# Token tiles transposed in chunks of two, three and four, with the first value projection following them, in a hybrid attention step

## The chip, the cores and the metric

The kernel runs on one core of a Trainium2 chip. The metric is the device time of one execution in microseconds; less is better.

## The reference

One decoder layer for a prompt of 1024 tokens with 16 meta tokens ahead of it, and for 8 samples of 4 new tokens each; 2048 features, all in 32-bit floats. Cut to what matters here, with the head of the layer in full:

```python
def rms_norm(x, g):
    var = mean(x * x, axis=-1)
    return x * rsqrt(var + 1e-6) * g

h = rms_norm(x, norm_pre_g)            # 16 + 1024 + 32 = 1072 tokens x 2048
u = h @ w_in                           # q, k, v, gate of 8 heads; q, k, v, gate, decay of 4 linear heads
...                                    # stick-breaking attention (prompt and paged samples),
...                                    # gated linear attention, SiLU gates
y = x + rms_norm(mixed @ w_out, norm_post_g)
```

The outputs are y for prompt and samples, the new keys and values, and the new linear states. The change is in how h is made, transposed and split, and in the value projection of the first attention head, `h @ w_in[:, 2048:2176]`.

## The kernel before

Every product with `w_in` is done in three matmuls with operands rounded to the fast 32-bit matmul format: a tensor is split into a rounded part (`hh`, `wh`) and the rest (`hl`, `wl`), and the products `wh*hh`, `wh*hl` and `wl*hh` are accumulated. The stationary operand is a weight block of 128 features by 128 outputs, the moving one is `h` transposed: features on partitions, tokens along columns. So `h` must first be normalized with tokens on partitions, and then transposed on TensorE.

The 1072 tokens are nine tiles: x0 (16 meta tokens and 112 of the prompt), x1 to x7 (128 each), x8 (the last 16 of the prompt and the 32 of the samples, with the two halves of the features on different partitions of one buffer). A tile is loaded as two halves of 1024 features (`load_x`, L198 on; 11 buffers) and normalized (`norm_x`, L217 on): ScalarE squares it with a running sum (L227; halves of 1024 for tiles 0 to 4, pieces of 512 after them, 256 for x8), VectorE adds the partial sums (L229), then `rstd_` (L154 on) takes the root: one VectorE operation, Ln and Exp on ScalarE (L162, L163), and four VectorE operations that refine it (L164 to L167). L238 scales the two halves in place.

The head then runs over three chunks of tokens, `CHUNKS`, of three tiles each. In each chunk, for each of the 16 blocks k of features, TensorE transposes the three tiles' blocks into one PSUM bank (`tx`, L262, five banks), ScalarE evacuates it, multiplied by the gain `gpre`, as `hh` (L263), and VectorE evacuates the rest as `hl` (L264). After a chunk's loop the 48 matmuls of the first head's value projection on the chunk follow in the program (L274 to L276), into one of three accumulators, `first`. Their token chunks, `SCHUNKS`, are 378, 378 and 316 columns, cut at multiples of 126 as the attention wants them, and stay within what has been transposed so far. The table `NORMS` places a tile's `norm_x` behind a step (c, k): x3 behind (0, 1), x4 behind (0, 4), x5 (0, 10), x6 (1, 2), x7 (1, 5), x8 (1, 8).

The weights of that projection come in four chunks of 256 KB (`weight_chunk`): ScalarE casts a chunk (L185, L182), VectorE subtracts (L187, L183). The raw chunks share two buffers with those of all later projections.

The order on each engine is drawn up at compile time by a list scheduler that goes by program order and its own estimate of when operands are there. Blocks marked `urgent()` (loads, casts, copies out of accumulators) go ahead of the rest. Each engine then works through its list in order and waits where an operand is late. Loads go through SP's queue and in small part ScalarE's, each of them in order too; eight semaphores take turns in telling of a load's landing, so that a load waits until the one eight before it has landed. `gpre` is a transposed load of 2048 single elements on ScalarE's queue, and the sixth load issued.

After the head, `head(0)` copies the three accumulators to staging tiles `vraw` (L613), which are written out later, and `inproj` runs the key and query projections, attention, the other heads and so on.

Of the kernel before, what the change touches and what calls it, by code (L numbers as in the profile page):

```python
# [20 lines left out]
P = 128  # L21
# [61 lines left out]
def hybrid_step(ctx: ExitStack, tc: tile.TileContext, x_prompt, x_sample, cache_k, cache_v, state_gla,  # L83
# [7 lines left out]
    def urgent():  # L91
        return tc.high_priority(offset=URGENT)
# [16 lines left out]
    def stage(nm, dt=F32):  # L109
        return stg.tile([P, 384], dt, tag="stg", name=nm)  # L110
# [44 lines left out]
    def rstd_(pl, ssq, n, rows, w, nm):  # L155

        v = pl.tile([P, w], F32, tag="rs_v", name=f"v_{nm}")
        r = pl.tile([P, w], F32, tag="rs_r", name=f"r_{nm}")
        t = pl.tile([P, w], F32, tag="rs_t", name=f"t_{nm}")
        v, r, t = v[:rows], r[:rows], t[:rows]  # L160
        vec.tensor_scalar(v, ssq, 1.0 / n, EPS, ALU.mult, ALU.add)
        act.activation(r, v, AF.Ln)  # L162
        act.activation(r, r, AF.Exp, scale=-0.5)  # L163
        vec.tensor_tensor(t, r, r, ALU.mult)  # L164
# [8 lines left out]
    hl = [t[:, 1088:1088 + T] for t in hT]  # L173


    def weight_chunk(w, kk, c0, nm, dst=None):
        with urgent():
            raw = wp.tile([P, 4, P], F32, tag="wr", name=f"wr_{nm}")
            nc.sync.dma_start(raw[:], w[kk * 512:(kk + 1) * 512, c0:c0 + P].rearrange("(k p) c -> p k c", p=P))
            wh, wl = dst or [wp.tile([P, 4, P], F32R, tag=t, name=f"{t}_{nm}") for t in ("wh", "wl")]  # L180
            if dst is None:
                act.copy(wh[:], raw[:])  # L182
                vec.tensor_tensor(wl[:], raw[:], wh[:].bitcast(F32), ALU.subtract)  # L183
                return [(wh[:, k, :], wl[:, k, :]) for k in range(4)]
            act.copy(wh, raw[:])  # L185
            for i in range(2):
                vec.tensor_tensor(wl[i][:], raw[:, 2 * i:2 * i + 2], wh[:, 2 * i:2 * i + 2].bitcast(F32), ALU.subtract)  # L187
        return [(wh[:, k, :], wl[k // 2][:, k % 2, :]) for k in range(4)]
# [3 lines left out]
    with tc.tile_pool(name="xp", bufs=2) as xp, tc.tile_pool(name="xps", bufs=5, space=PSUM) as xps:  # L192
        wf = xp.tile([P, 12, P], F32R, tag="wf", bufs=1, name="wf")
        wfl = [stg.tile([P, 2, P], F32R, tag="stg", name=f"wfl{kk}") for kk in range(6)]
        first = [accp.tile([P, 512], F32, tag="acc", name=f"acc_v0_{c}") for c in range(3)]
        wchunks = []
        xts = {}

        def load_x(i):

            xt = [xp.tile([P, H], F32, tag="x", bufs=11, name=f"x{i}_{f}") for f in range(2 if i < 8 else 1)]
            if i == 8:
                pool.memset(xt[0][32:64], 0.0)
            with urgent():
                for f in range(2):
                    fs = slice(f * H, (f + 1) * H)
                    if i == 0:
                        nc.scalar.dma_start(xt[f][:META], meta_tokens[:, fs])
                        nc.sync.dma_start(xt[f][META:], x_prompt[0, 0:P - META, fs])
                    elif i == 8:  # L210
                        nc.scalar.dma_start(xt[0][64 * f:64 * f + 16], x_prompt[0, SEQ - 16:SEQ, fs])
                        nc.sync.dma_start(xt[0][64 * f + 16:64 * f + 48], x_sample.rearrange("b t d -> (b t) d")[:, fs])
                    else:
                        nc.sync.dma_start(xt[f][:], x_prompt[0, i * P - META:(i + 1) * P - META, fs])
            xts[i] = xt

        def norm_x(i):  # L217
            xt = xts[i]
            rows = P if i < 8 else 112
            w = H if i < 5 else 512 if i < 8 else 256  # L220
            q = len(xt) * H // w
            ssq = xp.tile([P, 4], F32, tag="ssq", name=f"ssq{i}")
            for e in range(q):
                j0 = 0 if i < 5 else (448 if i < 8 else 768) + 1088 * (e % 2)
                jk = hT[15][:rows, j0:j0 + w]
                xe = xt[e * w // H][:rows, e * w % H:e * w % H + w]
                act.activation(jk, xe, AF.Square, accum_out=ssq[:rows, e:e + 1])  # L227
            sq = xp.tile([P, 1], F32, tag="sq", name=f"sq{i}")
            vec.tensor_reduce(sq[:rows], ssq[:rows, :q], mybir.AxisListType.X, ALU.add)  # L229
            if i == 8:  # L230
                other = xp.tile([P, 1], F32, tag="so", bufs=1, name="so")
                pool.memset(other[:], 0.0)
                vec.tensor_copy(other[0:48], sq[64:112])
                vec.tensor_copy(other[64:112], sq[0:48])
                vec.tensor_tensor(sq[:rows], sq[:rows], other[:rows], ALU.add)
            r = rstd_(xp, sq[:rows], D, rows, 1, f"x{i}")
            for t in xt:
                vec.tensor_scalar(t[:rows], t[:rows], r, None, ALU.mult)  # L238

        NORMS = {(0, 1): 3, (0, 4): 4, (0, 10): 5, (1, 2): 6, (1, 5): 7, (1, 8): 8}  # L240
        for i in range(5):
            load_x(i)
            if i == 2:
                constants()
                for kk in range(NK // 4):
                    dst = (wf[:, 4 * kk:4 * kk + 4, :], wfl[2 * kk:2 * kk + 2]) if kk < 3 else None
                    wchunks.extend(weight_chunk(w_in[0], kk, C_SV, f"v0_{kk}", dst))
        for i in range(3):
            norm_x(i)
        for c, (lo, hi) in enumerate(CHUNKS):  # L250
            n = hi - lo
            for k in range(NK):
                ps = xps.tile([P, 384], F32, tag="tx", name=f"tx{c}_{k}")
                ks = slice(k % 8 * P, (k % 8 + 1) * P)
                for j in range(3):
                    xt = xts[3 * c + j]
# [5 lines left out]
                    nc.tensor.transpose(ps[:, j * P:min((j + 1) * P, n)], src, ii)  # L262
                act.activation(hh[k][:, lo:hi], ps[:, :n], AF.Copy, scale=gpre[:, k:k + 1])  # L263
                vec.scalar_tensor_tensor(hl[k][:, lo:hi], ps[:, :n], gpre[:, k:k + 1], hh[k][:, lo:hi].bitcast(F32),  # L264
                                         ALU.mult, ALU.subtract)
                if c == 0 and k == 7:
                    load_x(5)
                if (c, k) in NORMS:
                    norm_x(NORMS[c, k])
            lo, hi = SCHUNKS[c]  # L270
            o_ = first[c][:, :hi - lo]
            for k in range(NK):
                wh, wl = wchunks[k]
                mm(o_, wh, hh[k][:, lo:hi], start=(k == 0), stop=False)  # L274
                mm(o_, wh, hl[k][:, lo:hi], start=False, stop=False)
                mm(o_, wl, hh[k][:, lo:hi], start=False, stop=(k == NK - 1))  # L276
            if c == 0:
                for i in (6, 7, 8):
                    load_x(i)

    def inproj(c0, evac, lo0, nm, chunks=CHUNKS):

# [191 lines left out]
    with tc.tile_pool(name="sp", bufs=1) as sp, tc.tile_pool(name="sps", bufs=1, space=PSUM) as sps:  # L474
# [135 lines left out]
        def head(h):  # L610
# [999 lines left out]
```

## Time and profile before

| | |
|---|---|
| median of 3 runs | 2091.61 us (2091.23 to 2092.55) |
| profiled execution | 2091.43 us |
| its span | 2089.6 us |
| TensorE (PE) busy in the span | 2050.1 us, 98% |
| VectorE (DVE) | 1554.0 us, 74% |
| ScalarE (ACT) | 962.7 us, 46% |
| DMA | 301.86 MB, 144 GB/s on average |

The span is what the profiler sees of the core; 1.8 us of the execution's time lie around it. Times of rows are in microseconds from the span's start. L numbers are lines of the kernel before. PE is TensorE's matmul side, PEld its weight loads, which overlap it; a matmul's row has its own duration, so that back-to-back matmuls overlap in the rows and their spacing is what one costs. "[1.72 <-ACT wf L185]" at a row's end means that the engine stood idle for 1.72 us before it, and what ended that.

### The profile page before, as it was taken

How to read it: one execution, taken by the hardware profiler on the slowest of the kernel's cores; microseconds unless marked ns; L12 is line 12 of the kernel's file. 1: busy time of each engine (PE TensorE's matmuls, PEld its weight loads, DVE VectorE, ACT ScalarE, POOL GpSimd, SP SyncE). 2: the span in 40 equal slices, each digit the busy share in tenths (PEclk: the TensorE clock that was granted, in tenths of full speed). 3: DMA queues.
4: the chain of work that ended last, by engine and by line, in shares of the span. 5: the costliest groups of instructions: out<-in, count | busy, mean ns of one | idle time of the engine just before them, and what ended most of it. 6: DMA issues, size and time to landing. Idle time of an engine off the chain costs nothing.

```text
span 2089.6 us, 42075 instructions
## 1 busy us (share of the span) xinstructions
PE 2050.1 (98%) x12546; PEld 1863.7 (89%) x12546; DVE 1554.0 (74%) x6299; ACT 962.7 (46%) x2304; POOL 84.3 (4%) x303
## 2 busy tenths in 40 slices
PE   5999999999999999999999999999999999999998
PEld 4999999999999998999899998998888897777776
DVE  6368889889888989899798887978444347553576
ACT  7345555565655556433535335353433325432332
POOL 0012000001000000000000000000000000000000
PEclk9999999999999999999999999999999999999999
DMA  6245554545554442533333434335777666442385
GB/s 204 78 139 150 145 151 137 168 129 153 144 157 142 138 126 77 144 95 85 107 98 81 118 78 115 90 85 159 229 238 227 224 215 194 137 151 75 129 280 186
DMA packets 374910, 301.86 MB, mean 144 GB/s; under 512 B 46488, under 2 KB 315192, under 8 KB 374680
## 3 DMA queue, kind: packets, MB, share of 16 engines
q1 hardware_dynamic: 372344, 298.64, 48.3%
q8 instruction: 99, 1.62, 0.3%
q14 instruction: 131, 1.07, 0.2%
q10 hardware_dynamic: 2336, 0.53, 0.1%
HBM read 241.75 MB, written 57.31 MB: 143 GB/s over the span
## 4 chain that ended last, share of the span: by engine, by line
PE 85%; DVE 8%; DMA 4%; issue 2%; ACT 1%; SPq 0%; POOL 0%; DVEq 0%; ACTq 0%; POOLq 0%
PE acc_g L292 5%; PE acc_g L293 5%; PE acc_g L294 5%; PE b L1517 4%; PE b L1518 4%; PE b L1519 4%; PE acc_k L292 3%; PE acc_k L293 3%; PE acc_k L294 3%; PE acc_v L292 3%; PE acc_q L292 3%; PE acc_q L293 3%; PE acc_q L294 3%; PE acc_v L294 3%; PE acc_v L293 3%; DVE jk L411 2%
## 5 line engine op out<-in xcount | busy, mean ns | idle before, releaser
L411 DVE SCALAR_TENSOR_TENSOR jk<-kp,qb 128x128 f32<-128x128 f32 x2048 | 591.7, 289 | 42.5 <-DMA qb<-qsd 1.5
L292 PE MATMUL acc_g<-hT,wh_g 128*128 128x368 f32 (+2 forms) x768 | 251.1, 327 | 0.0
L293 PE MATMUL acc_g<-hT,wh_g 128*128 128x368 f32 (+2 forms) x768 | 247.4, 322 | 0.0
L294 PE MATMUL acc_g<-hT,wl_g 128*128 128x368 f32 (+2 forms) x768 | 247.0, 322 | 0.0
L1517 PE MATMUL b<-ring,f 128*128 128x512 f32 x416 | 166.0, 401 | 4.0 <-DVE u L1399 1.6
L1335 DVE TENSOR_TENSOR ring<-wr,ring 128x512 fp32r<-128x512 f32 x104 | 70.7, 690 | 132.0 <-ACT ring L1334 131.6
L411 DVE DVE_READ_ACCUMULATOR jk<-kp,qb 128x1 f32 x2048 | 166.3, 81 | 0.0
L1518 PE MATMUL b<-ring,f 128*128 128x512 f32 x416 | 162.8, 391 | 0.3 <-DVE ring L1335 0.2
L1519 PE MATMUL b<-ring,f 128*128 128x512 f32 x416 | 162.9, 392 | 0.0
L292 PEld LDWEIGHTS acc_g<-hT,wh_g 128*128 128x128 f32 x768 | 144.3, 188 | 12.3 <-issue 10.6
L293 PEld LDWEIGHTS acc_g<-hT,wh_g 128*128 128x128 f32 x768 | 144.4, 188 | 1.5 <-issue 0.8
L294 PEld LDWEIGHTS acc_g<-hT,wl_g 128*128 128x128 f32 x768 | 144.3, 188 | 0.4 <-DVE wl_g L183 0.3
L1334 ACT CAST ring<-wr 128x512 fp32r<-128x512 f32 x104 | 64.2, 621 | 167.5 <-DMA wr<-in_w_out_dram 74.1
L292 PE MATMUL acc_gv<-hT,wh_gv 128*128 128x384 f32 (+1 forms) x384 | 129.9, 338 | 0.0
L292 PE MATMUL acc_k<-hT,wh_k 128*128 128x378 f32 (+1 forms) x384 | 127.6, 332 | 0.0
L293 PE MATMUL acc_k<-hT,wh_k 128*128 128x378 f32 (+1 forms) x384 | 125.4, 326 | 0.0
L292 PE MATMUL acc_q<-hT,wh_q 128*128 128x368 f32 (+2 forms) x384 | 125.4, 326 | 0.0
L294 PE MATMUL acc_k<-hT,wl_k 128*128 128x378 f32 (+1 forms) x384 | 125.2, 326 | 0.0
L294 PE MATMUL acc_gv<-hT,wl_gv 128*128 128x384 f32 (+1 forms) x384 | 124.5, 324 | 0.0
L293 PE MATMUL acc_gv<-hT,wh_gv 128*128 128x384 f32 (+1 forms) x384 | 124.5, 324 | 0.0
L293 PE MATMUL acc_q<-hT,wh_q 128*128 128x368 f32 (+2 forms) x384 | 123.6, 322 | 0.0
L294 PE MATMUL acc_q<-hT,wl_q 128*128 128x368 f32 (+2 forms) x384 | 123.5, 322 | 0.0
(441 smaller groups left out, 5301.7 us busy)
## 6 DMA issues: line engine op xcount, KB each, us to landing
kp<-in_cache_k_dram SPq DMA_DIRECT2D x512, 64.0 KB
vr<-in_cache_v_dram SPq DMA_DIRECT2D x64, 512.0 KB
tf<-in_w_out_dram SPq DMA_DIRECT2D x64, 256.0 KB
td<-tf SPq DMA_DIRECT2D x64, 256.0 KB
qb<-qsd SPq DMA_DIRECT2D x64, 256.0 KB
wr_g<-in_w_in_dram SPq DMA_DIRECT2D x64, 256.0 KB
wr<-td SPq DMA_DIRECT2D x64, 256.0 KB
wr<-in_w_out_dram SPq DMA_DIRECT2D x48, 256.0 KB
```

Of the source, the lines that this page charges most:

```text
L292: mm(acc[c][:, :n], wh, hh[k][:, lo:hi], start=(k == 0), stop=False)
L293: mm(acc[c][:, :n], wh, hl[k][:, lo:hi], start=False, stop=False)
L294: W.mark = mm(acc[c][:, :n], wl, hh[k][:, lo:hi], start=False, stop=(k == NK - 1)).ins
L411: ins = vec.scalar_tensor_tensor(jk[:], kp[:], 1.0, qbs[h, b][:, t, :], ALU.mult, ALU.mult, accum_out=zt[:, t, NPG - 1 - i:NPG - i])
L1334: act.copy(wh, r)
L1335: vec.tensor_tensor(wl, r, wh.bitcast(F32), ALU.subtract)
L1517: mm(bk[:], ah, wh, start=first and k == 0, stop=False, skip_group_check=True)
L1518: mm(bk[:], ah, wl, start=False, stop=False, skip_group_check=True)
L1519: mm(bk[:], al, wh, start=False, stop=last and k == 7, skip_group_check=True)
```

## The change

`XCHUNKS` takes the place of `CHUNKS` in the head: tiles (0, 1), (2, 3, 4), (5, 6, 7, 8), that is 256, 384 and 432 columns. The first head's value accumulators have these widths too, and are put together to the chunks of 126 in the copies to `vraw`, five copies for three. A token tile gets 13 half-tile buffers for 11. The raw tiles of the first two weight chunks get buffers of their own, and the first chunk's cast is put behind tile x1's root. The loads are issued in another order: x0, x1, weight chunk 0, x2, chunk 1, x3, chunks 2 and 3, x4, the constants, x5, then x6 behind step (0, 7) and x7 and x8 behind (0, 15).

In `norm_x` all squares are taken on a half of 1024 features (x8: its one buffer); x0's second half is squared by VectorE, and x1's squares stand behind x0's root. The root is shorter: two VectorE operations add the partial sums with the mean's factor and epsilon, Ln and Exp follow, two more VectorE operations make the correction, and the scaling multiplies by the raw root and the correction in one instruction. `NORMS` places x2 behind (0, 1), x3 (0, 6), x4 (0, 11), x5 (1, 1), x6 (1, 4), x7 (1, 8), x8 (1, 11). x0 and x1 are normalized ahead of the chunks.

```diff
+TILES = [(0, 1), (2, 3, 4), (5, 6, 7, 8)]
+XCHUNKS = [(0, 2 * 128), (2 * 128, 5 * 128), (5 * 128, T)]
...
-    def weight_chunk(w, kk, c0, nm, dst=None):
+    def weight_chunk(w, kk, c0, nm, dst=None, raw=None, behind=None):
         with urgent():
-            raw = wp.tile([P, 4, P], F32, tag="wr", name=f"wr_{nm}")
+            if raw is None:
+                raw = wp.tile([P, 4, P], F32, tag="wr", name=f"wr_{nm}")
...
-            act.copy(wh, raw[:])
+            ins = act.copy(wh, raw[:]).ins
+            if behind is not None:
+                tc.add_manual_dep(ins, behind.name, NOSYNC, reason="behind")
...
-            xt = [xp.tile([P, H], F32, tag="x", bufs=11, name=f"x{i}_{f}") for f in range(2 if i < 8 else 1)]
+            xt = [xp.tile([P, H], F32, tag="x", bufs=13, name=f"x{i}_{f}") for f in range(2 if i < 8 else 1)]
...
-            w = H if i < 5 else 512 if i < 8 else 256
-            q = len(xt) * H // w
-            ssq = xp.tile([P, 4], F32, tag="ssq", name=f"ssq{i}")
+            q = len(xt)
+            ssq = xp.tile([P, 2], F32, tag="ssq", name=f"ssq{i}")
+            jk = hT[15][:].rearrange("p (a x) -> p a x", a=2)[:rows, :, 576:1088]
             for e in range(q):
-                j0 = 0 if i < 5 else (448 if i < 8 else 768) + 1088 * (e % 2)
-                jk = hT[15][:rows, j0:j0 + w]
-                xe = xt[e * w // H][:rows, e * w % H:e * w % H + w]
-                act.activation(jk, xe, AF.Square, accum_out=ssq[:rows, e:e + 1])
-            sq = xp.tile([P, 1], F32, tag="sq", name=f"sq{i}")
-            vec.tensor_reduce(sq[:rows], ssq[:rows, :q], mybir.AxisListType.X, ALU.add)
+                x, s = xt[e][:rows], ssq[:rows, e:e + 1]
+                if i == 0 and e == 1:
+                    vec.scalar_tensor_tensor(hT[14][:, 0:H], x, 1.0, x, ALU.mult, ALU.mult, accum_out=s)
+                else:
+                    ins = act.activation(jk, x.rearrange("p (a x) -> p a x", a=2), AF.Square, accum_out=s).ins
+                    if i == 1:
+                        tc.add_manual_dep(ins, roots[0].name, NOSYNC, reason="behind")
...
-            r = rstd_(xp, sq[:rows], D, rows, 1, f"x{i}")
-            for t in xt:
-                vec.tensor_scalar(t[:rows], t[:rows], r, None, ALU.mult)
-
-        NORMS = {(0, 1): 3, (0, 4): 4, (0, 10): 5, (1, 2): 6, (1, 5): 7, (1, 8): 8}
...
+            vec.tensor_scalar(t, ssq[:rows, 0:1], 1.0 / D, EPS, ALU.mult, ALU.add)
+            vec.scalar_tensor_tensor(v, second, 1.0 / D, t, ALU.mult, ALU.add)
+            act.activation(g, v, AF.Ln)
+            roots.append(act.activation(g, g, AF.Exp, scale=-0.5).ins)
+            vec.scalar_tensor_tensor(t, g, v, g, ALU.mult, ALU.mult)
+            vec.tensor_scalar(t, t, -0.5, 1.5, ALU.mult, ALU.add)
+            for x in xt:
+                vec.tensor_scalar(x[:rows], x[:rows], g, t, ALU.mult, ALU.mult)
+
+        def load_w(kk):
+            dst = (wf[:, 4 * kk:4 * kk + 4, :], wfl[2 * kk:2 * kk + 2]) if kk < 3 else None
+            raw = xp.tile([P, 4, P], F32, tag="wx", name=f"wx{kk}") if kk < 2 else None
+            wchunks.extend(weight_chunk(w_in[0], kk, C_SV, f"v0_{kk}", dst, raw, roots[1] if kk == 0 else None))
+
+        roots = []
+        NORMS = {(0, 1): 2, (0, 6): 3, (0, 11): 4, (1, 1): 5, (1, 4): 6, (1, 8): 7, (1, 11): 8}
+        LOADS = {(0, 7): (6,), (0, 15): (7, 8)}
+        for i in (0, 1):
+            load_x(i)
+        norm_x(0)
+        norm_x(1)
+        load_w(0)
+        load_x(2)
+        load_w(1)
+        load_x(3)
+        load_w(2)
+        load_w(3)
+        load_x(4)
+        constants()
+        load_x(5)
+        for c, (lo, hi) in enumerate(XCHUNKS):
...
-            lo, hi = SCHUNKS[c]
             o_ = first[c][:, :hi - lo]
...
                 for c, (lo, hi) in enumerate(SCHUNKS):
-                    with urgent():
-                        ev_v(c, first[c][:, :hi - lo], lo, hi)
+                    raw = stage(f"vraw{h}_{c}")
+                    for i, (a, b) in enumerate(XCHUNKS):
+                        s, e = max(a, lo), min(b, hi)
+                        if s < e:
+                            with urgent():
+                                act.copy(raw[:, s - lo:e - lo], first[i][:, s - a:e - a])
+                    W.spawn(tok_out(raw, c, lo, hi, h, new_v_prompt, new_v_sample, f"v{h}"))
```

More of the change, by code (lines that the diff above doesn't have):

```diff
@@ L219, in norm_x @@
             rows = P if i < 8 else 112
[L220 to L222 removed]
+            q = len(xt)
+            ssq = xp.tile([P, 2], F32, tag="ssq", name=f"ssq{i}")
+            jk = hT[15][:].rearrange("p (a x) -> p a x", a=2)[:rows, :, 576:1088]
             for e in range(q):
[L224 to L229 removed]
+                x, s = xt[e][:rows], ssq[:rows, e:e + 1]
[5 more added lines that the diff above has]
+                        tc.add_manual_dep(ins, roots[0].name, NOSYNC, reason="behind")
+            v, g, t = [xp.tile([P, 1], F32, tag=f"rs_{n}", name=f"{n}_x{i}")[:rows] for n in "vgt"]
             if i == 8:
@@ L248, in hybrid_step @@
-        for i in range(3):
-            norm_x(i)
-        for c, (lo, hi) in enumerate(CHUNKS):
+                vec.tensor_copy(other[0:48], ssq[64:112, 0:1])
+                vec.tensor_copy(other[64:112], ssq[0:48, 0:1])
+                second = other[:rows]
+            else:
+                second = ssq[:, 1:2]
+            vec.tensor_scalar(t, ssq[:rows, 0:1], 1.0 / D, EPS, ALU.mult, ALU.add)
+            vec.scalar_tensor_tensor(v, second, 1.0 / D, t, ALU.mult, ALU.add)
+            act.activation(g, v, AF.Ln)
@@ L254, in hybrid_step @@
                 ks = slice(k % 8 * P, (k % 8 + 1) * P)
-                for j in range(3):
-                    xt = xts[3 * c + j]
+                for j, i in enumerate(TILES[c]):
+                    xt = xts[i]
                     if len(xt) == 2:
@@ L265, in hybrid_step @@
                                          ALU.mult, ALU.subtract)
-                if c == 0 and k == 7:
-                    load_x(5)
+                for i in LOADS.get((c, k), ()):
+                    load_x(i)
                 if (c, k) in NORMS:
                     norm_x(NORMS[c, k])
-            lo, hi = SCHUNKS[c]
             o_ = first[c][:, :hi - lo]
```

14 lines of the change are left out of this document (1 added, 13 removed).

## The prediction

> **What bounds the kernel now.** First the page, for the whole span, then busy time by stretches of the span, to see where TensorE is not full.
>
> ```profile
> span 2089.6 us, 42075 instructions
> PE 2050.1 (98%) x12546; PEld 1863.7 (89%) x12546; DVE 1554.0 (74%) x6299; ACT 962.7 (46%) x2304; POOL 84.3 (4%) x303
> 0.00:72.00 72.00, 50.98 (x292) 41.98 (x293) 48.26 (x133) 50.91 (x128) 2.74 (x16) 1.00 0.50 150
> 72.00:400.00 328.00, 326.70 (x1989) 313.86 (x1988) 255.74 (x1112) 168.32 (x400) 34.85 (x119) 1.00 0.50 143
> ```
>
> In a window's row stand the stretch, its length, then PE, PEld, DVE, ACT and POOL busy, granted clock, DMA share and GB/s. TensorE is busy 98% of the whole, and 326.70 of the 328 us behind the first 72; in those 72 it misses 21. What shifts the start of the steady part shifts the end of the kernel by as much. The change touches only what lies ahead of it, so the question is one time: when does the first matmul of the key projection start? Here it is 71.32 us (below). The next rows split the head into its stages.
>
> ```profile
> 0.00:13.10 13.10, 0.00 (x0) 0.02 (x1) 1.91 (x10) 7.57 (x16) 1.38 (x10) 1.00 0.86 265
> 13.10:20.70 7.60, 3.73 (x15) 2.76 (x15) 6.34 (x21) 5.36 (x12) 0.00 (x0) 1.00 0.76 221
> 20.70:41.30 20.60, 17.67 (x98) 14.26 (x96) 17.37 (x45) 17.05 (x46) 1.04 (x1) 1.00 0.90 268
> 41.30:57.60 16.30, 15.18 (x96) 13.02 (x96) 14.67 (x41) 12.86 (x40) 0.00 (x0) 1.00 0.00 0
> 57.60:71.30 13.70, 13.70 (x82) 11.21 (x82) 7.96 (x18) 7.44 (x16) 0.32 (x5) 1.00 0.02 5
> ```
>
> From 20.7 to 57.6 us VectorE is busy 0.84 and then 0.90 of the time, ScalarE 0.83 and 0.79: these two pace the head. In the last stage each has over 40% of its time free, and TensorE paces. What turns the one into the other is the last token tile, x8: the third chunk's transposes need it scaled. The chain of waits (first two rows) and the timeline have the start, this handover and the end.
>
> ```profile
> 1.77 16.39 DMA gpre<-in_norm_pre_g_dram
> 18.17 0.33 SPq L214
> 14.35 1.41 DVE L238 TENSOR_SCALAR x<-x,r_x 128x1024 f32<-128x1024 f32 x2
> 20.11 1.05 ACT L263 ACTIVATE hT<-tx,gpre 128x384 fp32r<-128x384 f32 x2 [0.96 <-PE tx L262]
> 53.41 0.20 ACT L163 ACTIVATE r_x<-r_x 112x1 f32<-112x1 f32 x1
> 55.33 0.76 DVE L238 TENSOR_SCALAR x<-x,r_x 112x1024 f32<-112x1024 f32 x1
> 55.56 2.14 PE L262 MATMUL tx<-ident,x 128*128 128x128 f32 x14
> 57.63 0.41 PE L274 MATMUL acc_v<-hT,wf 128*128 128x316 f32 x1
> 71.32 0.33 PE L292 MATMUL acc_k<-hT,wh_k 128*128 128x378 f32 x1
> ```
>
> So now: evacuations begin at 20.11, x8 is scaled at 55.33 + 0.76 = 56.09, and the tail from there to 71.32 takes 15.2. gpre, the gain that every evacuation multiplies by, lands at 1.77 + 16.39 = 18.16, before the change and after it: no evacuation can precede that.
>
> **What the change does to the start.** Now the first evacuation waits for x2 to be scaled and transposed (20.11). After the change x0 and x1 suffice, and x1 is scaled at 15.76 even now; so gpre ends last. Its transfer is not touched, and the same loads (tiles 0 to 3, two weight chunks) are issued ahead of the first one that waits for its semaphore, which SP issues at 18.17: x4's first half now, w2 then. I take 18.16. That gains 1.9 here, and makes the shortening of x0's and x1's own chain worth nothing. x0's second square moves to VectorE, in a form that this trace lacks; its nearest rows are two-source ones (the second is from the groups by line):
>
> ```profile
> 23.59 0.76 DVE L187 TENSOR_TENSOR wfl<-wr_v,wf 128x256 fp32r<-128x256 f32 x2 [1.72 <-ACT wf L185]
> L183 DVE TENSOR_TENSOR wl_v<-wr_v,wh_v 128x512 fp32r<-128x512 f32 x1 | 0.7, 692 | 0.7 <-ACT wh_v L182 0.7
> ```
>
> 0.38 at 256 columns and 0.69 at 512 give 1.3 at 1024. Anything from 0.7 to 2 is hidden: VectorE is busy 1.91 of the first 13.1 us and the result is not due before gpre. The two new "behind" edges hold x1's squares and w0's cast on ScalarE until a root is taken; in its queue behind them stand w1's cast and the squares of x2 and x3. Their cover is again gpre; if it is gone, it is the slower rival below.
>
> **VectorE's work up to x8.** Prices are the spacings of equal instructions in a row, where there are such:
>
> ```profile
> 36.68 2.17 DVE L264 SCALAR_TENSOR_TENSOR hT<-tx,gpre,hT 128x384 fp32r<-128x384 f32 x4
> 57.15 3.32 DVE L264 SCALAR_TENSOR_TENSOR hT<-tx,gpre,hT 128x304 fp32r<-128x304 f32 x7 [1.07 <-ACT hT L263]
> 12.26 1.42 DVE L238 TENSOR_SCALAR x<-x,r_x 128x1024 f32<-128x1024 f32 x2
> L894 DVE TENSOR_SCALAR ow<-ow,r_g,t_g 128x256 f32<-128x256 f32 x32 | 13.2, 413 | 1.2
> L909 DVE TENSOR_SCALAR ow_s<-ow_s,r_g_s 128x256 f32<-128x256 f32 x8 | 2.8, 348 | 0.0
> 26.18 0.15 DVE L164 TENSOR_TENSOR t_x<-r_x 128x1 f32<-128x1 f32 x1
> 26.25 0.61 DVE L264 SCALAR_TENSOR_TENSOR hT<-tx,gpre,hT 128x384 fp32r<-128x384 f32 x1
> ```
>
> An evacuation costs 0.54 at 384 columns and 0.47 at 304, so 0.43 at 256 and 0.58 at 432. Scaling half a tile costs 0.71. The shorter root leaves two per-partition factors to that instruction; L894 against L909 (two factors against one, same shape) puts the second at 0.065, so 0.775. The bounds are 0.71 and, at the two-source price, 1.3; L894 is nearest, being the same operation. A root's small operation holds VectorE for 0.07 (26.18 to 26.25); each tile has four for six.
>
> From the first evacuation until x8 is scaled VectorE now does 32 x 0.54 + 11 half tiles x 0.71 + three weight splits 2.1 + 39 small ones x 0.07 = 29.9, in the 36.0 us from 20.11 to 56.09. After the change, from 18.16: 16 x 0.43 for the two-tile chunk, 12 x 0.54 of the second (x8's norm stands behind its twelfth step), 11 x 0.775, four splits 2.9 (w1's too, as the stage starts earlier), 26 x 0.07: together 26.6. Evacuations give 3.9 of it, since more of them move behind x8; the second factor and the split take part of that back.
>
> How densely VectorE is packed decides the rest: 0.84 in the first stage, 0.90 in the second. The 1.72 in the L187 row above is a wait of the first stage: a weight chunk that landed late.
>
> ```profile
> 22.94 0.62 ACT L185 CAST wf<-wr_v 128x512 fp32r<-128x512 f32 x1 [1.78 <-DMA wr_v<-in_w_in_dram]
> ```
>
> w2 travels behind half of x4 now; after the change it is the first load behind gpre, with evacuations ready to run meanwhile. So I take 0.90: 26.6 / 0.90 = 29.6, and x8 is scaled at 18.16 + 29.6 = 47.7. Its data come in time: some 5.6 MB (by their shapes) are left at 18.2, 21 us at the 268 GB/s of the third stage, so landed at 39; two more token buffers let x5 and half of x6 be issued without a release.
>
> **ScalarE** has to keep up:
>
> ```profile
> 8.85 1.06 ACT L227 ACTIVATE hT<-x 128x1024 fp32r<-128x1024 f32 x1 [0.16 <-DMA x<-in_x_prompt_dram]
> 9.90 0.19 ACT L162 ACTIVATE r_x<-v_x 128x1 f32<-128x1 f32 x1
> 37.45 0.62 ACT L227 ACTIVATE hT<-x 128x512 fp32r<-128x512 f32 x1
> 38.06 0.62 ACT L227 ACTIVATE hT<-x 128x512 fp32r<-128x512 f32 x1
> 49.32 2.98 ACT L263 ACTIVATE hT<-tx,gpre 128x384 fp32r<-128x384 f32 x6
> ```
>
> A square of 1024 takes 1.05 of its queue, two of 512 take 1.22. An evacuation takes 0.50 at 384; scaled as VectorE's, 0.40 at 256. To x8's root it has 16 x 0.40 + 12 x 0.50 + 11 x 1.05 + four casts x 0.62 + 12 x 0.1 = 27.6, VectorE's amount in the same 29 us. That is tight, and the reason for the rivals.
>
> **The tail becomes longer.** TensorE's prices:
>
> ```profile
> 44.41 0.34 PE L275 MATMUL acc_v<-hT,wf 128*128 128x378 f32 x1
> 44.58 0.49 PE L262 MATMUL tx<-ident,x 128*128 128x128 f32 x3
> 44.83 0.42 PE L276 MATMUL acc_v<-hT,wfl 128*128 128x378 f32 x1
> 45.08 0.49 PE L262 MATMUL tx<-ident,x 128*128 128x128 f32 x3
> ```
>
> A matmul of 378 columns takes 0.17, three transposes 0.25 and 0.08 more on the matmul behind them, so 0.11 each. The 13.69 us from 57.63 to 71.32 hold 48 matmuls of 316 columns (0.144 at that rate, 6.9 together) and eleven groups of three transposes, 0.62 each. After the change matmuls of 432 take 0.197, 9.5 together, and a group has one transpose more: 11 x 0.73 = 8.0. With the 1.5 from x8's scaling to 57.63 (the first banks' transposes) the tail is 19.0 for 15.2. The columns together are the same 1072: work moved, not added.
>
> **Sum.** 47.7 + 19.0 = 66.7 for 71.32: 4.6 us earlier. The copies out of the accumulators are five for three; one of 378 takes
>
> ```profile
> L613 ACT COPY vraw<-acc_v 128x378 f32<-128x378 f32 x2 | 0.9, 474 | 0.0
> ```
>
> so the two behind the last accumulator take under 0.9, and the key projection needs it only after twelve matmuls, 2.1 us; without that cover, under 0.5 more than now. The profiled execution took 2091.43 us (the span and 1.8 around it); the median, 2091.61, is 0.2 above. Forecast: 2091.6 - 4.6 = 2087.0 us.
>
> **Rivals.**
> *TensorE paces throughout.* Matmuls can start at 18.6. The first chunk holds 32 transposes less ten done, 22 x 0.11, and 48 matmuls of 256, x 0.117: 8.0; the second 48 x 0.11 + 48 x 0.175 = 13.7; the third 9.5 + 16 x 0.69 = 20.5: 60.8. They begin slow:
>
> ```profile
> 22.41 0.52 PE L276 MATMUL acc_v<-hT,wfl 128*128 128x378 f32 x1
> 25.52 0.34 PE L276 MATMUL acc_v<-hT,wfl 128*128 128x378 f32 x1
> ```
>
> 0.52 against 0.34 for the same matmul; the slow stretch is over by 25.5, so about 2 are lost: 62.8, 8.5 us gained, 2083.1. TensorE's stalls in the third stage speak for it, VectorE's 0.90 against it. [...]
>
> *Nothing gained.* All 16 evacuations of the second chunk slip in ahead of x8's scaling, as they do now, and VectorE stays at 0.84: 28.8 / 0.84 = 34.3, x8 at 52.5, end at 71.5, 2091.8. For it: both engines are near full, and each small operation of a root waits behind an evacuation. Against it: the wait for w2 goes.
>
> *Slower: ScalarE's queue stands still on gpre.* x1 being scaled early, the first evacuation can stand in ScalarE's in-order queue ahead of the squares of x2 and x3 and of w1's cast. These then wait for 18.16 as well: 27.6 + 2.1 (x2) + 2.0 (four evacuations more, as above) = 31.7, at its 0.83 of now 38.2, x8's root at 56.4, scaled 2.7 later as now (53.41 to 56.09): 59.1 + 19.0 = 78.1, 6.8 us slower, 2098.4. It decides when all four halves are unsquared at 18.2; with two, the case above results.
>
> **Chances.** Forecast 0.42, TensorE pacing 0.15, nothing gained 0.25, slower 0.18. About 4.2 us (0.2%) is what a measurement here can tell from no change. The forecast lies just beyond, so 0.05 of its chance counts as within: faster 0.52, same 0.30, slower 0.18. The range, 2082 to 2096, leaves out the slower rival's full size and takes in a scaled half tile at its bound of 1.3 (11 x 0.52 / 0.90 = 6.4 later, 2093.4); the forecast's own is 2085 to 2090, from a packing of 0.95 (1.6 earlier) to 16 evacuations ahead of x8 (2.4 later).
>
> **What would show it.** Right: the first evacuation at 18.2; x8 scaled near 47.7 and the first key matmul near 66.7; VectorE 0.90 busy between. Wrong: gpre landing elsewhere; squares of x2 or x3 behind the first evacuation; a scaled half tile far over 0.8; a tail other than 19; or a stage behind the head that loses what the head gains.

## The result, and the profile after

The changed kernel takes 2088.53 us (median of 22 runs, 2085.94 to 2092.8) where the kernel before takes 2092.05 beside it (22 runs, 2089.25 to 2095.55): ratio 0.9983, 95% interval 0.9977 to 0.9990, some 3.5 us (2.1 to 4.8) less. The forecast was 4.6 less. Single executions of one kernel differ by several us, so what follows reads the head in the traces, where it repeats to 0.14 us (e1), and uses the times to confirm.

The page of the changed kernel (from here on, L numbers are lines of the kernel that ran):

```profile
span 2088.5 us, 42049 instructions
PE 2050.6 (98%) x12546; PEld 1864.7 (89%) x12546; DVE 1553.9 (74%) x6282; ACT 960.1 (46%) x2286; POOL 84.8 (4%) x303
```

Busy time by stretches (stretch, length, PE, PEld, DVE, ACT, POOL, granted clock, DMA share, GB/s): the changed kernel's head and the 328.7 us behind its first key matmul, then its head by stages.

```profile
0.00:68.10 68.10, 50.19 (x288) 42.41 (x289) 47.27 (x116) 47.20 (x107) 3.18 (x16) 1.00 0.54 159
68.10:396.80 328.70, 327.63 (x1995) 314.81 (x1995) 255.86 (x1112) 169.39 (x402) 34.92 (x119) 1.00 0.51 143
...
15.50:31.10 15.60, 12.99 (x81) 12.22 (x81) 13.63 (x40) 15.31 (x39) 1.48 (x1) 1.00 1.00 363
31.10:49.00 17.90, 15.64 (x97) 13.23 (x98) 16.90 (x43) 14.29 (x35) 0.00 (x0) 1.00 0.34 70
49.00:68.10 19.10, 18.93 (x104) 15.11 (x103) 10.48 (x19) 9.99 (x19) 0.32 (x5) 1.00 0.03 8
```

The kernel before, the same 328.7 us behind its own first key matmul:

```profile
71.30:400.00 328.70, 327.40 (x1993) 314.56 (x1992) 255.74 (x1112) 168.95 (x401) 34.85 (x119) 1.00 0.50 143
```

TensorE does the same 327.5 us of work in both: this stretch of the steady part is unaltered, and the head is 3.2 us shorter. The two profiled spans differ by only 1.1 us: from the first key matmul to the end it is 2018.3 us before and 2020.4 after, and from 2017.3 to 2022.9 over all the traces here. So a single span doesn't show what a head is worth; the medians agree with it. The head's marks, from the timeline of the changed kernel:

```profile
15.53 0.47 ACT L288 ACTIVATE hT<-tx,gpre 128x256 fp32r<-128x256 f32 x1 [0.81 <-DMA gpre<-in_norm_pre_g_dram]
48.21 0.81 DVE L252 TENSOR_SCALAR x<-x,g_x,t_x 112x1024 f32<-112x1024 f32 x1
68.11 0.33 PE L313 MATMUL acc_k<-hT,wh_k 128*128 128x378 f32 x1
```

The first evacuation still waits for gpre, but at 15.53, not 18.16. x8 is scaled at 49.02 and the first key matmul comes at 68.11 (before: 20.11, 56.09, 71.32). In the first stage ScalarE is busy 0.98, in the second VectorE 0.94; in the last TensorE has no gap to speak of.

One account turned out to hold for all kernels below. TensorE's busy time by a stretch between the first evacuation and the first key matmul (stretch, length, PE, clock, DMA share, GB/s; so too in all later rows of this kind), before:

```profile
20.11:71.32 51.21, 47.16 (x277) 1.00 0.38 113
```

and after:

```profile
15.53:68.11 52.58, 47.57 (x278) 1.00 0.42 134
```

So the first key matmul = first evacuation + some 47 us of TensorE work, if its clock holds, + its idle time. The columns to be worked off are the same in both. The 3.21 us gained are 4.58 of earlier start, less 1.37 of more idle and busy time together. How the 1.37 splits differs from trace to trace: idle 0.96 and busy 0.41 more in this one, idle 1.48 more and busy 0.26 less in e1.

### The profile page after: what moved, and what is told of

Its sections match the earlier page's. It is cut to its first block, busy times and chain, and to the rows that moved or that the text cites. A ratio compares the mean times of both kernels' runs of the same rounds, so it can differ in the third digit from the quotient of the medians.

```text
span 2088.5 us, 42049 instructions
## 1 busy us (share of the span) xinstructions
PE 2050.6 (98%) x12546; PEld 1864.7 (89%) x12546; DVE 1553.9 (74%) x6282; ACT 960.1 (46%) x2286; POOL 84.8 (4%) x303
## 3 DMA queue, kind: packets, MB, share of 16 engines
q8 instruction: 99, 1.62, 0.3%
## 4 chain that ended last, share of the span: by engine, by line
PE 84%; DVE 7%; DMA 4%; issue 2%; ACT 1%; SPq 0%; POOL 0%; DVEq 0%; ACTq 0%; POOLq 0%
PE acc_g L313 5%; PE acc_g L314 5%; PE acc_g L315 5%; PE b L1543 4%; PE b L1544 4%; PE b L1545 4%; PE acc_k L313 3%; PE acc_k L314 3%; PE acc_k L315 3%; PE acc_q L313 3%; PE acc_q L314 3%; PE acc_q L315 3%; PE acc_v L313 3%; DVE jk L432 3%; PE acc_v L315 2%; PE acc_v L314 2%
## 5 line engine op out<-in xcount | busy, mean ns | idle before, releaser
L313 PEld LDWEIGHTS acc_g<-hT,wh_g 128*128 128x128 f32 x768 | 144.3, 188 | 12.4 <-issue 10.6
```

Source lines behind the costliest of these rows:

```text
L313: mm(acc[c][:, :n], wh, hh[k][:, lo:hi], start=(k == 0), stop=False)
```

## Experiments

All edits are to the changed kernel. The table has, from each trace, the first evacuation, x8 scaled, the first key matmul, TensorE's busy and idle time from the first to the third, and the ratio of its times to those of the kernel before.

| kernel | evac. | x8 | key | busy | idle | ratio, 95% interval |
|---|---|---|---|---|---|---|
| before | 20.11 | 56.09 | 71.32 | 47.16 | 4.05 | 1 |
| after | 15.53 | 49.02 | 68.11 | 47.57 | 5.01 | 0.9983, 0.9977 to 0.9990 |
| e1 again | 15.55 | 48.88 | 67.98 | 46.90 | 5.53 | one run |
| e2 equal chunks | 20.67 | 51.54 | 69.70 | 46.45 | 2.58 | 0.9991, 0.9982 to 1.0000 |
| e3 x8 early | 15.47 | 46.00 | 73.16 | 50.67 | 7.02 | 1.0003, 0.9994 to 1.0012 |
| e4 flat gain | 14.82 | 48.27 | 67.35 | 48.56 | 3.97 | 0.9984, 0.9975 to 0.9993 |
| e5 weights later | 18.24 | 52.10 | 71.22 | 47.98 | 5.00 | 0.9996, 0.9986 to 1.0007 |
| e6 x8 early, filled | 15.57 | 46.11 | 71.79 | 48.75 | 7.47 | 1.0008, 0.9998 to 1.0017 |
| e7 GpSimd scales | 15.51 | 48.76 | 67.94 | 47.38 | 5.05 | 0.9978, 0.9968 to 0.9988 |
| e8 warm | 16.68 | 48.93 | 69.66 | 46.91 | 6.07 | 0.9977, 0.9967 to 0.9988 |
| e9 long roots | 15.56 | 51.25 | 70.11 | 48.79 | 5.76 | 0.9999, 0.9983 to 1.0015 |
| e10 short squares | 15.47 | 51.12 | 78.66 | 55.63 | 7.56 | 1.0035, 1.0020 to 1.0050 |
| e11 flat, in order | 15.68 | 52.48 | 73.20 | 49.87 | 7.65 | 1.0010, 1.0001 to 1.0019 |
| e12 eleven buffers | 15.48 | 49.08 | 69.81 | 47.79 | 6.54 | 0.9991, 0.9981 to 1.0002 |

**e1, the changed kernel again**, nothing edited.

> The changed kernel once more, for its trace alone. If the head is repeatable, the first evacuation (15.53 in the first trace), the end of x8's scaling (49.02) and the first key matmul (68.11) come back within 0.3 us, and these three times can be compared between single traces, although whole executions differ by some 2 us from run to run.

The marks repeat within 0.14 us, in this one repetition; busy and idle time only within 0.7. The two traces show why: TensorE's equal matmuls of 256 columns halve their spacing at 24.1 us in the first trace and at 22.6 in this one. So TensorE has 0.67 us less of busy time here, waits 0.52 longer, and the key matmul comes only 0.13 sooner. What follows compares marks; differences of under 0.7 in busy or idle time alone show nothing.

**e2, chunks of three tiles**, all else as changed:

```diff
-TILES = [(0, 1), (2, 3, 4), (5, 6, 7, 8)]
+TILES = [(0, 1, 2), (3, 4, 5), (6, 7, 8)]
...
-        NORMS = {(0, 1): 2, (0, 6): 3, (0, 11): 4, (1, 1): 5, (1, 4): 6, (1, 8): 7, (1, 11): 8}
+        NORMS = {(0, 1): 3, (0, 4): 4, (0, 10): 5, (1, 2): 6, (1, 5): 7, (1, 8): 8}
...
         load_x(2)
+        norm_x(2)
```

> The changed kernel with three equal chunks of three tiles (384, 384, 304 columns), norms placed as in the kernel before, everything else kept. Theory (the head's end is x8's scaling plus TensorE's tail, and x8's scaling is VectorE's and ScalarE's work at a packing of 0.9): all 32 evacuations of 384 come ahead of x8, 1.9 us more than now, and the first waits for x2 again; x8 at 51 to 54, tail 15.2, first key matmul 66.5 to 69, so the split in itself is worth within 1.5 us of nothing. Rival (the split carries the gain): first key matmul at 70.5 to 72, as before the change.

Its timeline:

```profile
20.67 1.05 ACT L289 ACTIVATE hT<-tx,gpre 128x384 fp32r<-128x384 f32 x2 [0.50 <-PE tx L288]
50.74 0.80 DVE L252 TENSOR_SCALAR x<-x,g_x,t_x 112x1024 f32<-112x1024 f32 x1
69.70 0.34 PE L314 MATMUL acc_k<-hT,wh_k 128*128 128x378 f32 x1
```

x8 came in the range expected, the key matmul just past it: the tail was 18.2, not 15.2. The first evacuation waits for x2 again, 5.1 us later, and the key matmul is only 1.6 later, since TensorE, once started, waits for 2.6 us in place of 5.0. A short first chunk starts TensorE on work that does not last.

**e3, x8 early**: the norms of x5 to x8 called sooner.

```diff
-        NORMS = {(0, 1): 2, (0, 6): 3, (0, 11): 4, (1, 1): 5, (1, 4): 6, (1, 8): 7, (1, 11): 8}
+        NORMS = {(0, 1): 2, (0, 6): 3, (0, 11): 4, (0, 14): 5, (1, 0): 6, (1, 2): 7, (1, 4): 8}
```

> The changed kernel with the norms of x5 to x8 placed behind steps (0,14), (1,0), (1,2), (1,4) in place of (1,1), (1,4), (1,8), (1,11); nothing else. Theory (x8's scaling is the handover): x8 is scaled at 45 to 47 with 4 to 6 evacuations of 384 behind it, and the first key matmul comes 1.5 to 3 us earlier, 65 to 66.6. Rival (TensorE paces: the second chunk's matmuls and transposes, once late, are still to be done): x8 earlier but the first key matmul within 0.7 of 68.1.

Its timeline:

```profile
45.20 0.80 DVE L252 TENSOR_SCALAR x<-x,g_x,t_x 112x1024 f32<-112x1024 f32 x1
73.16 0.34 PE L313 MATMUL acc_k<-hT,wh_k 128*128 128x378 f32 x1
```

TensorE by stretches of its trace:

```profile
32.80:36.20 3.40, 2.04 (x11) 1.00 1.00 175
36.20:46.50 10.30, 8.75 (x35) 0.50 0.12 26
```

Neither theory foresaw this: x8 was scaled 3.0 us sooner, as meant, and the key matmul came 5.1 later. That refutes the prediction's chain, in which the tail follows x8 at a fixed distance (here 27.2). The squares of x5 to x8 stand ahead of evacuations on ScalarE; TensorE, waiting for those, was busy 2.04 of 3.40 us, and then its granted clock (the column behind its busy time) stood at 0.50 for 10.3 us.

**e4, flat gain**: the gain comes as 16 rows of 512 B, and TensorE transposes it.

```diff
-    act.dma_start(gpre[:], norm_pre_g[0].rearrange("(k p) -> p k", p=P), allow_slow_non_contiguous=True)
...
+            act.dma_start(gflat[:], norm_pre_g[0].rearrange("(k p) -> k p", p=P))
...
+        nc.tensor.transpose(pg[:, :NK], gflat[:], ident[:NK, :NK])
+        vec.tensor_copy(gpre[:], pg[:, :NK])
```

> The changed kernel with the gain loaded as 16 rows of 512 bytes and transposed by one TensorE instruction, so that it lands by about 5 us in place of 15.45 and no later load waits for it. Theory A (loads and the first evacuation pace): x3's load is issued at 10 to 11 in place of 15.47, the first evacuation comes at 14.7 in place of 15.53, x8 is scaled 2 to 3 us earlier, first key matmul 65 to 66. Theory B (VectorE's and ScalarE's packing alone paces): the start gains 0.8 and the end as much, 67.3.

Its timeline:

```profile
14.82 0.47 ACT L293 ACTIVATE hT<-tx,gpre 128x256 fp32r<-128x256 f32 x1 [0.31 <-PE tx L292]
67.35 0.33 PE L318 MATMUL acc_k<-hT,wh_k 128*128 128x378 f32 x1
```

Theory B: with the gain no longer waited for, x1's transposes are, 0.7 us earlier; the loads of x3 and x4, 5.4 us earlier at SyncE (10.08 for 15.47), bring no more. The key matmul is 0.76 earlier, and the times do not tell this from the changed kernel.

**e5, weights later**: chunk 1 is requested behind x2, chunks 2 and 3 behind x3.

```diff
+            if after is not None:
+                tc.add_manual_dep(d, after.name, NOSYNC, reason="behind")
...
-            wchunks.extend(weight_chunk(w_in[0], kk, C_SV, f"v0_{kk}", dst, raw, roots[1] if kk == 0 else None))
+            wchunks.extend(weight_chunk(w_in[0], kk, C_SV, f"v0_{kk}", dst, raw, roots[1] if kk == 0 else None, xdma[3] if kk > 1 else xdma[2] if kk else None))
```

> Weight chunk 1 is requested behind x2 and chunks 2 and 3 behind x3, the order that the prediction took for granted; all else as after. The gain gpre's 2,048 small packets then share the DMA engines with token tiles of 4 KB packets instead of weights of 512 B packets. Theory (what stands beside gpre in the engines decides when it lands): it lands at 17.5 to 18.7, as it did before the change, and the first evacuation starts then; the weights come later too, so that the first key matmul moves to 69 or later. Rival (gpre's landing hangs on its own packets alone): 15.2 to 15.8, first evacuation 15.5.

Its timeline:

```profile
18.24 0.84 ACT L291 ACTIVATE hT<-tx,gpre 128x256 fp32r<-128x256 f32 x2 [4.36 <-DMA gpre<-in_norm_pre_g_dram]
71.22 0.33 PE L316 MATMUL acc_k<-hT,wh_k 128*128 128x378 f32 x1
```

The theory held: the gain lands where it did before the change, and with it the head's gain is gone, 71.22 for 71.32.

**e6, e3 with filler**: the norms as in e3, and throwaway transposes keep TensorE busier.

```diff
...
+                NF = 3 if c == 1 and k < 8 else 0
+                for u in range(NF):
+                    nc.tensor.transpose(ps[:, 384:512], ident[:], ident[:])
```

> The early norms of e3 again, with three throwaway transposes of the identity (into a free quarter of the bank) behind each of the first eight transposed groups of the second chunk, so that TensorE is not left idle between 31 and 36 us. Theory (e3 lost its 2.8 us of earlier x8 to the clock: half speed from 36.0 to 46.3 because TensorE had stood too idle): the granted clock stays 1.00 from 31 to 49, the matmuls of 384 follow one another in 0.175, not 0.32, x8 is scaled at 45.5 to 46.7, the second chunk's matmuls end by 49, and the first key matmul comes at 66 to 68. Rival (ScalarE's squares put ahead of the evacuations hold TensorE back, whatever the clock): the second chunk's matmuls still end after 51 and the first key matmul comes at 70.5 or later.

Its timeline:

```profile
45.30 0.81 DVE L252 TENSOR_SCALAR x<-x,g_x,t_x 112x1024 f32<-112x1024 f32 x1
71.79 0.34 PE L316 MATMUL acc_k<-hT,wh_k 128*128 128x378 f32 x1
```

TensorE by stretches of its trace:

```profile
39.00:42.40 3.40, 1.91 (x12) 1.00 0.19 56
```

The clock stayed at 1.00 from its first record at 22.0 us through the head, and the key matmul still came 3.7 us behind that of the changed kernel. So the rival is right: with no fall of the clock, the evacuations held back by squares (idle 7.5) turn the gain of e3's earlier x8 into a loss. How e3's 5.1 us split is not settled: the filler is work too (busy 1.2 us more than in the changed kernel), so the clock's share is 1.4 us, the difference of the two kernels, or more.

**e7, GpSimd scales** the second halves of x2 to x7.

```diff
-            for x in xt:
-                vec.tensor_scalar(x[:rows], x[:rows], g, t, ALU.mult, ALU.mult)
+            for f, x in enumerate(xt):
+                eng = pool if f == 1 and i in (2, 3, 4, 5, 6, 7) else vec
+                eng.tensor_scalar(x[:rows], x[:rows], g, t, ALU.mult, ALU.mult)
```

> The second half of tiles x2 to x7 is scaled on GpSimd, not on VectorE: VectorE loses 6 x 0.765 = 4.6 us ahead of x8. Theory (VectorE's packed work sets when x8 is scaled, as the prediction has it): with half of that taken up by ScalarE, which is busy 0.98 to 31 us and 0.80 behind, x8 is scaled at 45 to 47.5 and the first key matmul comes at 64.5 to 66.8. Rival (ScalarE paces, or GpSimd is too slow or holds VectorE up): x8 at 48.3 or later, first key matmul at 67.4 or later.

Groups of its instructions between 15 and 50 us (count, busy, mean ns, idle before):

```profile
L253 POOL TENSOR_SCALAR x<-x,g_x,t_x 128x1024 f32<-128x1024 f32 x6 | 8.3, 1384 | 34.6 <-DVE t_x L250 22.1 <-ACT hT L289 6.0 <-ACT hT L233 3.6
L253 DVE TENSOR_SCALAR x<-x,g_x,t_x 128x1024 f32<-128x1024 f32 x6 | 7.9, 1316 | 0.1
```

The changed kernel's, there from 15.5 to 49 us:

```profile
L252 DVE TENSOR_SCALAR x<-x,g_x,t_x 128x1024 f32<-128x1024 f32 x12 | 9.2, 808 | 0.0
```

The rival held: VectorE scales six halves in place of twelve and saves 1.3 us, not 4.6. Its four that started behind GpSimd's took 1.48 to 1.62, the two that started first 0.81 each. What VectorE would do with half its scaling gone is therefore not shown.

**e8, warm**: 36 transposes of the identity ahead of the first real ones.

```diff
+                NF = 36 if c == 0 and k == 0 else 0
+                for u in range(NF):
+                    nc.tensor.transpose(ps[:, 384:512], ident[:], ident[:])
```

> 36 throwaway transposes of the identity ahead of the first real ones, so that TensorE has worked some 9 us before x0 is scaled. The first chunk's matmuls of 256 followed one another in 0.21 us up to 23.9 us and in 0.12 behind that, while the clock column said 1.00 throughout. Theory (ScalarE and VectorE pace this stretch, as the prediction has it): the matmuls follow in 0.12 from 16.6 on, TensorE stands idle for 2 us more up to 31, x8 is scaled within 0.5 of 49.0 and the first key matmul comes within 0.5 of 68.1. Rival (the slow TensorE holds the transposes and with them both evacuating engines): x8 at 46 to 48, the first key matmul at 65 to 67.

Its timeline:

```profile
69.66 0.34 PE L316 MATMUL acc_k<-hT,wh_k 128*128 128x378 f32 x1
```

TensorE by stretches of its trace:

```profile
7.30:11.80 4.50, 0.33 (x1) 1.00 1.09 340
11.80:22.00 10.20, 6.08 (x26) 0.50 1.06 313
```

The means failed: the filler did release the clock (its transposes follow one another in 0.21 us up to 4.9 and in 0.11 behind that), but it ended at 7.3, TensorE stood idle, and from 11.8 to 22.0 it was slow again. The order of its queue moved too. It tells nothing on what a warm start is worth; e1, with a release 1.5 us sooner and a key matmul 0.13 sooner, speaks for little. Its times are no worse than those of the changed kernel though its head is 1.6 longer. In its trace what lies behind the head is the shortest of all, 2017.3 us; why stays unexplained.

**e9, long roots**: the root of the kernel before.

```diff
...
+            r = rstd_(xp, sq[:rows], D, rows, 1, f"x{i}")
             for x in xt:
-                vec.tensor_scalar(x[:rows], x[:rows], g, t, ALU.mult, ALU.mult)
+                vec.tensor_scalar(x[:rows], x[:rows], r, None, ALU.mult)
```

> The root of before in after's kernel: sum of the squares, six tiny VectorE operations and one factor, where after has four and two factors. By the account that e1 to e8 suggest, the first key matmul comes at the first evacuation (15.5) plus some 47 us of TensorE work plus TensorE's idle time (5.0 in after); a part of the change matters as far as it alters one of the three. Theory (the longer root makes each tile later by about three tiny operations at 0.15 and puts TensorE's waits up): idle 5.5 to 6.5, first key matmul at 68.6 to 69.8. Rival (the tiny operations lie in gaps, and one factor is 0.05 cheaper a half tile): within 0.4 of 68.1.

Its timeline:

```profile
70.11 0.33 PE L308 MATMUL acc_k<-hT,wh_k 128*128 128x378 f32 x1
```

TensorE by stretches of its trace:

```profile
31.50:34.90 3.40, 2.00 (x14) 1.00 1.11 218
34.90:38.30 3.40, 3.40 (x16) 0.50 0.35 44
```

Later by 2.0 us, 0.3 past the theory's range. Idle time, 5.76, is in the range expected, but so are the 5.53 of e1, whose root is short: what the longer root in itself costs is not shown. What e9 has more is a stretch of 3.4 us at half clock, which adds up to 1.7 of busy time.

**e10, short squares**: ScalarE squares x5 to x7 in pieces of 512, x8 in pieces of 256.

```diff
+            w = H if i < 5 else 512 if i < 8 else 256
+            q = len(xt) * H // w
...
-                x, s = xt[e][:rows], ssq[:rows, e:e + 1]
+                x, s = xt[e * w // H][:rows, e * w % H:e * w % H + w], ssq[:rows, e:e + 1]
...
```

> The squares of before (512 wide from x5 on, 256 wide in x8) in after's kernel, with tiny VectorE operations that add their sums up. Before, 26 of them took 19.7 + 5.4 us of ScalarE ahead of the first key matmul, in after 16 take 16.9 + 3.1; all the extra lies on x5 to x8, some 3 us. Theory (ScalarE is a pacer next to VectorE): x8 is scaled 1 to 3 us later than 49.0 and the first key matmul comes at 69 to 71. Rival (ScalarE's free fifth between 31 and 49 us takes it up): within 0.4 of 68.1.

Its timeline:

```profile
50.31 0.81 DVE L259 TENSOR_SCALAR x<-x,g_x,t_x 112x1024 f32<-112x1024 f32 x1
```

TensorE by stretches of its trace:

```profile
49.80:53.30 3.50, 1.83 (x13) 0.99 0.00 0
53.30:73.70 20.40, 20.40 (x64) 0.50 0.00 1
73.70:78.70 5.00, 5.00 (x27) 1.00 0.11 31
```

x8 is scaled 2.1 us later, as the theory has it; the key matmul is 10.6 later. TensorE waited for x8, was busy 1.83 of 3.50 us, and then ran at half clock until 25 of the third chunk's 48 matmuls were left. The times agree: 2098.18, a ratio of 1.0035.

**e11, flat gain, squares in order**: the norms of x3 and x4 called sooner, the squares of x5 to x8 tied behind the evacuation at which they are called.

```diff
...
+                    if i >= 5:
+                        tc.add_manual_dep(ins, after.name, NOSYNC, reason="behind")
...
-        NORMS = {(0, 1): 2, (0, 6): 3, (0, 11): 4, (1, 1): 5, (1, 4): 6, (1, 8): 7, (1, 11): 8}
+        NORMS = {(0, 1): 2, (0, 5): 3, (0, 9): 4, (1, 0): 5, (1, 4): 6, (1, 8): 7, (1, 11): 8}
```

> The flat gain load of e4, the norms of x3 and x4 one and two evacuations earlier, and the squares of x5 to x8 held behind the evacuation at which they are called, so that none stands ahead of the second chunk's first evacuations on ScalarE (in e4 TensorE waited some 1.7 us there, at 30 to 34 us). Theory (first evacuation + 47 + idle): first evacuation 14.8, idle 2.5 to 3.3, first key matmul at 65.3 to 66.7. Rival (the squares only move the waits elsewhere, as in e3): idle 3.7 or more, first key matmul at 67.2 or later.

Its timeline:

```profile
73.20 0.34 PE L320 MATMUL acc_k<-hT,wh_k 128*128 128x378 f32 x1
```

TensorE by stretches of its trace:

```profile
25.90:29.30 3.40, 1.54 (x11) 1.00 0.87 296
29.30:32.70 3.40, 3.40 (x18) 0.50 0.98 220
```

The rival, and worse than it: the first evacuation came at 15.68, not 14.8, TensorE's wait at 30 to 34 us only came earlier, with a stretch at half clock behind it, x8 slipped to 52.48, and TensorE idled 7.65 us. An order written to close one gap opened others.

**e12, eleven token buffers** (13 to 11 in one line).

> Token buffers 11 in place of 13. Only the second half of x7 and x8 then have to wait for a buffer, behind the first loads of the key's weights in SyncE's queue. Theory (they land before ScalarE comes to square them, at 38 and 41.8): first key matmul within 0.4 of 68.1. Rival (x7 or x8 is late): x8 scaled at 49.6 or later, first key matmul at 68.7 or later.

Its timeline:

```profile
35.08 1.12 ACTq L216 DMA_DIRECT2D x<-in_x_prompt_dram  x2
36.25 1.06 ACT L233 ACTIVATE hT<-x 128x1024 fp32r<-128x1024 f32 x1 [0.91 <-DMA wr_k<-in_w_in_dram]
38.40 0.55 PE L287 MATMUL tx<-ident,x 128*128 128x128 f32 x3 [1.50 <-DVE hT L289]
69.81 0.34 PE L313 MATMUL acc_k<-hT,wh_k 128*128 128x378 f32 x1
```

TensorE by stretches of its trace:

```profile
15.48:69.81 54.33, 47.79 (x278) 1.00 0.41 128
```

Neither as told: x8 is scaled at 49.08, as with 13, and the key matmul is still 1.7 later; TensorE idled 6.54. With 11 buffers x8's two loads on ScalarE's queue (the first row, ACTq) go out at 35.08 to 36.20, with 13 at 30.87; the square behind them in that queue starts at 36.25 in place of 34.42, and TensorE then waits 1.50 us for an evacuation. x8's time alone does not say when the head ends.

No kernel is shown to beat the changed one: the intervals of e4, e7 and e8 all hold its ratio.

## Why the forecast was nearly right

The time came 1.5 us above the forecast; the gain lies within the 4.2 us that the forecast took for the bound of a measurement, though 22 runs of each kernel do tell it from none. The forecast said 66.7 for the first key matmul, and it came at 68.11. But two of its steps were wrong, in opposite directions. That they nearly cancelled is luck.

*gpre lands at 18.16 before and after: wrong.* It landed 2.7 us sooner. The step took the same loads to stand ahead of it, tiles 0 to 3 and two weight chunks. In fact all four weight chunks are now requested by 8.5 us (the new raw tiles of w0 and w1 need no release), and x3 goes out behind gpre, at 15.47; the scheduler even put w2 and w3 ahead of w0 and w1. e5 shows that this matters: with the chunks requested later, gpre lands at 18.2 and the head is as long as before. The DMA records show how: while gpre is on its way, about one of its 4-byte packets passes for each packet of the other queue. From 8 to 9 us, among mostly 4 KB packets, 105 of its packets pass beside 104; from 9 to 10, among mostly 512 B ones, 350 beside 347. The weights travel in packets of 512 B, the tokens in 4 KB: with more weights beside it, gpre's 2,048 packets pass sooner.

*VectorE's work up to x8, 26.6 us: too little.* It was 13.63 + 16.90 = 30.5 in the two stages. All 16 evacuations of the second chunk went ahead of x8, not 12 (4 x 0.54 = 2.2), and x2's two half tiles fall behind the first evacuation, since this came early (2 x 0.765 = 1.5). The packing, 0.90, was right: 30.5 / 33.5 = 0.91. (Measured in the same way it was already 0.89 before, 31.9 of 36.0 us; the prediction's own list for before, 29.9, is 2.0 short of that.) So x8 was scaled at 49.02 for 47.7: 2.6 us of earlier start against 3.9 of longer way. In e5, where gpre lands at 18.2 and the weights come later too, the rival "nothing gained" comes true: x8 at 52.10 and the key matmul at 71.22; the rival said 52.5 and 71.5.

*The prices* were right. From the changed kernel's groups up to the first key matmul:

```profile
L289 DVE SCALAR_TENSOR_TENSOR hT<-tx,gpre,hT 128x256 fp32r<-128x256 f32 x16 | 7.1, 477 | 0.6 <-ACT hT L288 0.6
L231 DVE SCALAR_TENSOR_TENSOR hT<-x 128x1024 fp32r<-128x1024 f32 x1 | 1.2, 1225 | 7.6 <-DMA x<-in_x_prompt_dram 7.6
```

An evacuation of 256 columns holds VectorE for 7.1 / 16 = 0.44 (0.43 forecast), x0's second square takes 1.23 (1.3), a half tile with two factors 9.2 / 12 = 0.77 (0.775).

*The tail of 19.0* measured 19.09, but as a law it is wrong. It held where TensorE had started the last matmul of the second chunk when x8 came (e4, e5, e7: 19.1 to 19.2). Where five of them were still to come it was 20.7 (e8, e11, e12), with 25 of them 25.7 (e6), and with half clock over 27 (e3, e10). x8's scaling is a mark on the way; what ends the head is TensorE's start, work and idle time.

*The rivals.* "TensorE paces throughout" was wrong with 5.0 us of idle time, yet its view, work counted from the first evacuation, is the one that holds. "ScalarE stands still on gpre" did not happen: ScalarE waited 0.81 us for it, though x2's second square did end up behind four evacuations (it started at 18.02).

*The parts.* With the rest of the change in place, undoing one makes the first key matmul later by 1.6 (chunks), 2.0 (roots), 10.6 (squares; 8.1 of it is more busy time, from the half clock), 1.7 (buffers), 3.1 (weight requests). Each alone takes half of the 3.2 us or more, so the parts do not add up: in three of these five kernels TensorE waits longer (roots, squares, buffers), and in two its clock falls (roots, squares).

## What to carry to other kernels

Before a head is costed as a chain ending at its last input, count the pacing engine's work from its first to its last instruction there and ask only what alters its start and its idle time; an input that comes sooner at the price of a gap earlier on gains nothing. Read from the trace in which order loads were requested, weights included, before a small transfer's landing is taken as fixed. And price a gap on TensorE at more than its length: here 1.4 us of short gaps close together were followed by half clock worth up to 1.7 us (e9), and 1.7 us of them by 8.1 us (e10).

## What the chip showed unasked

**Half clock behind short gaps.** In e3, e9, e10 and e11 the clock fell to 0.50 behind some 3.4 us in which TensorE was busy 0.45 to 0.60; no gap in them exceeded 1.8 us. By the clock's records the slow stretches last one (e9, e11: 3.4 us), three (e3: 10.3) or six (e10: 20.4) times 3.41 us, which is the length of the single ones near the end of the kernels before and after (below). Busy share alone does not decide: 1.70 of 3.40 us in e5 (29.3 to 32.7) and 1.91 in e6 (39.0 to 42.4) passed without a fall. Nor does it decide the release: e10 stayed slow for 20.4 us with TensorE busy throughout by its records. What is counted stays open.

**The clock column starts late.** In the changed kernel it reads 1.00 from the start, while matmuls of 256 followed one another in 0.21 us until 23.9 and in 0.12 afterwards; the first record of the clock is at 24.1. At the start the spacing of equal matmuls is to be trusted, not the column.

**Spells far from the head.** Single slow stretches also stand near the end, where nothing was altered: 3.41 us at a clock of 0.50 from 1997.9 us in the kernel before, from 2031.2 in the changed one. Busy time by stretches, TensorE alone, of the kernel before:

```profile
1990.00:2002.00 12.00, 10.50 (x48) 0.86 0.80 266
```

and of the changed kernel:

```profile
2020.00:2036.00 16.00, 13.44 (x53) 0.89 0.90 297
```

Their place differs from trace to trace (e1 has one at 1460 us, e2 none). 3.41 us at half clock cost up to 1.7, by an estimate (half of it), which can be a part of why executions of one kernel differ by several us.

**Two engines scaling at once.** e7's pairs show VectorE's scaling at 0.81 when it starts first and about 1.55 when GpSimd has started: it ends only behind the other. VectorE's four end 0.55 us behind GpSimd's, and GpSimd's take 1.75 when VectorE has started first, 1.20 otherwise. Why one holds up the other no trace here shows.
